# The second block's modulation: sums over partitions by PE transposes and a DVE reduction, two sums in one tied group

## The chip, the cores and the metric

The kernel runs on one core of one Trainium2 chip. The metric is the device time of one launch in microseconds, the median of several runs. The engines are named as the profile does: PE (TensorE matmuls), PEld (its weight loads), DVE (VectorE), ACT (ScalarE), POOL (GpSimd), SP (which starts most DMAs).

## What is computed

Two blocks of two layers each run one after the other over 256 tokens of width 1024, all in fp32. The first block's layers have four mixing branches and a gated feed-forward network. The second block's layers are modulated: the shift, scale and gate vectors come from a conditioning vector `c`, and not from the tokens.

```python
def second_block(x, c, ctx, c_ctx, mod_w, mod_b, ...):
    silu_c = jax.nn.silu(c)                      # (1, 1024)
    silu_cc = jax.nn.silu(c_ctx)
    for i in range(DEPTH):                       # DEPTH = 2
        sh1, sc1, g1, sh2, sc2, g2 = jnp.split((silu_c @ mod_w[i] + mod_b[i])[:, None, :], 6, axis=-1)
        a = modulate(h, norm1_w[i], sh1, sc1)
        if ctx_read:                             # layer 0 alone
            csh1, csc1, cg1, csh2, csc2, cg2 = jnp.split(silu_cc @ mod_w[i] + mod_b[i], 6, axis=-1)
            ac = modulate(hc, norm1_w[i], csh1, csc1)
        ...
```

`mod_w[i]` is 1024 x 6144, so `silu_c @ mod_w[i]` is a product of one row with a large matrix. Only this product is touched here. The context needs the first 2048 of its 6144 columns.

## The kernel before

The kernel is one straight program without loops on the chip. It is recorded operation by operation in Python and then ordered by a scheduler, which weighs every engine's work by a cost model and assigns each instruction its place on its engine's queue. Every queue runs in the order so found. Thus a change to a few instructions can move others far away, on every engine.

Large matrix products (`s_tiles`, `t_form`, with `mm3`) are made of three matmuls each, with weights and tokens split into a high and a low part (lines 483 to 485 and 519 to 521). `weights` (lines 454 to 479) fetches the weights as tiles `w` of 128x1024 (512 KB), ACT casts them to `wh` (line 469) and DVE subtracts to get `wl` (line 470). There are four buffers for `w` and three each for `wh` and `wl`, so these engines can prepare weights ahead of PE.

The product with `mod_w` is made otherwise, beside the first block. `b2_setup` (line 1233) is a generator, and `pump` takes a step of it at each group of matmuls that the first block records, at a rate that depends on the place. It calls `mod_vec` (line 1198): for a block `b` of 512 output columns, eight slices `mw` of `mod_w` (128 rows x 512 columns, two to a DMA) are each multiplied on DVE by a column of `cs`, which holds `silu_c`, and added up in `macc` (lines 1216 and 1218). What is then left is the sum of `macc` over its 128 partitions, and this is wanted as columns: element 128 m + p of the block on partition p, in column m. PE makes it with four matmuls (line 1224), a 128x128 piece of `macc` as weights and one column of ones, into a bank of PSUM, and DVE adds the bias into `mod` or `modc` (line 1226).

There are three calls: layer 0, columns 0 to 2047, for both `c` and the context's vector (four blocks, two accumulators each, `macc0` and `macc1`); layer 0, the other eight blocks, `c` alone (`macc0` alone); layer 1, twelve blocks, `c` alone (`macc0` alone). This makes 28 sums.

The bank comes from `aux2`, of which there are two. The first block takes banks of `aux2` too, for its memory branch (`br_m`) and for the broadcast of the norm's factor (`rstd_bcast`). `macc` buffers are single, so that a block can begin to accumulate in one only when the sum has read it.

At the border of two layers the next layer's norm (lines 437 to 440: `nt`, then `hh` on ACT and `hl` on DVE) needs all of `xT`, so that its first matmuls can't be prepared further ahead than their weights.

Of the kernel before, what the change touches and what calls it, by code (L numbers as in the profile page):

```python
# [3 lines left out]

# [6 lines left out]
F32 = mybir.dt.float32  # L11
# [4 lines left out]
OP = mybir.AluOpType  # L16
AX = mybir.AxisListType
# [231 lines left out]
class K:  # L249
# [948 lines left out]
    def mod_vec(self, i, vecs, blocks, lp):  # L1198

        nc = self.nc  # L1200
        w = self.A["t_mod_w_2"][i]
        for b in blocks:
            accs = [lp.tile([128, 512], F32, tag=f"macc{j}", bufs=1, name="macc") for j in range(len(vecs))]
            for k0 in range(0, KT, 2):
                if k0:
                    yield
                v = lp.tile([128, 2, 512], F32, tag="mw", bufs=2, name="mw")
                self.later(v[:, 0, :1])
                c = TILE_AT["mod_w_2", b * 512][0] + k0 * 128 * 512
                nc.sync.dma_start(v.rearrange("p k n -> p (k n)"),  # L1210
                                  w[c:c + 256 * 512].rearrange("(p n) -> p n", p=128))
                for k in range(2):
                    for acc, (cv, _) in zip(accs, vecs):
                        sc = cv[:, k0 + k:k0 + k + 1]
                        if k0 + k == 0:
                            nc.vector.tensor_scalar(acc, v[:, k, :], sc, None, op0=OP.mult)
                        else:
                            nc.vector.scalar_tensor_tensor(acc, v[:, k, :], sc, acc, op0=OP.mult, op1=OP.add)  # L1218
            yield
            for acc, (_, out) in zip(accs, vecs):  # L1220
                with self.banks("aux2"):
                    ps = self.aux()
                for m in range(4):
                    nc.tensor.matmul(ps[:, m:m + 1], acc[:, m * 128:(m + 1) * 128], self.ones[:, :1], start=True,  # L1224
                                     stop=True)
                nc.vector.tensor_tensor(out[:, b * 4:b * 4 + 4], ps[:, :4], self.col("mod_b_2", i * 48 + b * 4, 4),
                                        OP.add)

    def gain(self, name, i, sc, dst):
        nc = self.nc  # L1230
# [1042 lines left out]
```

## Time and profile before

| | us |
|---|---|
| median of three runs | 1944.95 (1944.28 to 1946.02) |
| the profiled execution | 1944.3 |
| its span, first to last instruction | 1942.5 |
| PE busy | 1905.6 (98%) |
| weight loads busy | 1859.7 (96%) |
| DVE busy | 1479.6 (76%) |
| ACT busy | 1050.7 (54%) |
| granted TensorE clock, mean | 0.994 |

A busy time is the union of an engine's records. Matmul records overlap: each is some 0.28 us long, but the starts of two are about 0.12 us apart, and it is the distance of the starts that tells what one costs in a full stream. A row that stands for several records in a timeline gives their union. A wait is idle time of an engine, put down to what ended last before it went on.

### The profile page before, as it was taken

How to read it: one execution, taken by the hardware profiler on the slowest of the kernel's cores; microseconds unless marked ns; L12 is line 12 of the kernel's file. 1: busy time of each engine (PE TensorE's matmuls, PEld its weight loads, DVE VectorE, ACT ScalarE, POOL GpSimd, SP SyncE). 2: the span in 40 equal slices, each digit the busy share in tenths (PEclk: the TensorE clock that was granted, in tenths of full speed). 3: DMA queues.
4: the chain of work that ended last, by engine and by line, in shares of the span. 5: the costliest groups of instructions: out<-in, count | busy, mean ns of one | idle time of the engine just before them, and what ended most of it. 6: DMA issues, size and time to landing. Idle time of an engine off the chain costs nothing.

```text
span 1942.5 us, 39726 instructions
## 1 busy us (share of the span) xinstructions
PE 1905.6 (98%) x16234; PEld 1859.7 (96%) x16234; DVE 1479.6 (76%) x2362; ACT 1050.7 (54%) x1642; POOL 119.0 (6%) x120
## 2 busy tenths in 40 slices
PE   7999999999999999999999999998999999999998
PEld 7999999999999999999999999997899999899998
DVE  5988987896776879977778966887775557997554
ACT  6664455564644774454555544765254446555443
POOL 0102000110001001000000000000110000010001
PEclk9999999999999999999999999999999999999999
DMA  8865755966567766756653536443146666535653
GB/s 314 290 220 196 243 188 184 308 237 215 182 226 240 266 213 206 242 166 212 244 186 117 188 115 209 150 152 112 63 153 203 195 189 208 178 112 188 193 190 123
DMA packets 118759, 379.63 MB, mean 195 GB/s; under 512 B 18755, under 2 KB 28784, under 8 KB 117296
## 3 DMA queue, kind: packets, MB, share of 16 engines
q1 hardware_dynamic: 117808, 376.44, 57.7%
q8 instruction: 127, 2.08, 0.4%
q0 software_dynamic: 768, 0.66, 0.1%
q14 instruction: 56, 0.46, 0.1%
HBM read 365.94 MB, written 10.25 MB: 194 GB/s over the span
## 4 chain that ended last, share of the span: by engine, by line
PE 88%; DVE 4%; ACT 3%; issue 2%; DMA 1%; POOL 0%; SPq 0%; DVEq 0%; POOLq 0%; ACTq 0%
PE mm L485 23%; PE mm L483 23%; PE mm L484 23%; DVE wl L470 1%; ACT wh L469 1%; PE mm L519 1%; PE aux L1224 1%; PE mm L520 1%; PE mm L521 1%; PE aux L2123 1%; PE aux L2106 1%; PE aux L859 1%; DMA mw<-in_t_mod_w 1%; PE aux L483 1%; PE aux L485 1%
## 5 line engine op out<-in xcount | busy, mean ns | idle before, releaser
L469 ACT CAST wh<-w 128x1024 fp32r<-128x1024 f32 (+2 forms) x570 | 589.0, 1035 | 626.9 <-PE mm L484 473.6
L470 DVE TENSOR_TENSOR wl<-w,wh 128x1024 fp32r<-128x1024 f32 (+2 forms) x570 | 684.4, 1202 | 280.3 <-ACT wh L469 277.7
L483 PE MATMUL mm<-hh,wh 128*128 128x256 f32 (+1 forms) x1776 | 499.9, 282 | 1.4 <-ACT bq L766 0.7
L485 PE MATMUL mm<-hh,wl 128*128 128x256 f32 (+1 forms) x1776 | 499.4, 282 | 1.2 <-DVE wl L470 1.0
L484 PE MATMUL mm<-hl,wh 128*128 128x256 f32 (+1 forms) x1776 | 498.5, 281 | 0.0
L485 PEld LDWEIGHTS mm<-hh,wl 128*128 128x128 f32 (+1 forms) x1776 | 332.6, 187 | 4.1 <-DVE wl L470 1.8
L483 PEld LDWEIGHTS mm<-hh,wh 128*128 128x128 f32 (+1 forms) x1776 | 332.7, 187 | 3.5 <-issue 1.0
L484 PEld LDWEIGHTS mm<-hl,wh 128*128 128x128 f32 (+1 forms) x1776 | 332.3, 187 | 2.4 <-issue 1.8
L485 PE MATMUL mm<-xh,wl 128*128 128x256 f32 x960 | 269.6, 282 | 1.5 <-DVE wl L470 1.5
L483 PE MATMUL mm<-xh,wh 128*128 128x256 f32 x960 | 267.9, 280 | 1.2 <-DVE dqT L1262 0.7
L484 PE MATMUL mm<-xl,wh 128*128 128x256 f32 x960 | 268.6, 281 | 0.2
L485 PE MATMUL mm<-ph,wl 128*128 128x256 f32 x704 | 196.4, 279 | 0.0
L483 PE MATMUL mm<-ph,wh 128*128 128x256 f32 x704 | 195.9, 278 | 0.0
L484 PE MATMUL mm<-pl,wh 128*128 128x256 f32 x704 | 195.8, 278 | 0.0
L485 PEld LDWEIGHTS mm<-xh,wl 128*128 128x128 f32 x960 | 181.1, 189 | 5.1 <-issue 2.6
L483 PEld LDWEIGHTS mm<-xh,wh 128*128 128x128 f32 x960 | 180.8, 189 | 4.1 <-issue 2.7
L484 PEld LDWEIGHTS mm<-xl,wh 128*128 128x128 f32 x960 | 180.6, 189 | 2.9 <-issue 2.2
L1218 DVE SCALAR_TENSOR_TENSOR macc<-mw,cs,macc 128x512 f32<-128x512 f32 x196 | 145.6, 747 | 14.0 <-DMA mw<-in_t_mod_w 13.1
L484 PEld LDWEIGHTS mm<-pl,wh 128*128 128x128 f32 x704 | 132.4, 188 | 0.0
L485 PEld LDWEIGHTS mm<-ph,wl 128*128 128x128 f32 x704 | 132.2, 188 | 0.1
L483 PEld LDWEIGHTS mm<-ph,wh 128*128 128x128 f32 x704 | 132.1, 188 | 0.0
L483 PE MATMUL mm<-brh,wh 128*128 128x256 f32 x384 | 107.9, 281 | 0.0
(705 smaller groups left out, 3478.6 us busy)
## 6 DMA issues: line engine op xcount, KB each, us to landing
w<-in_t_w_in SPq DMA_DIRECT2D x148, 512.0 KB
w<-in_t_ffn_w SPq DMA_DIRECT2D x128, 512.0 KB
mw<-in_t_mod_w SPq DMA_DIRECT2D x96, 512.0 KB
w<-in_t_ffn_w_up SPq DMA_DIRECT2D x88, 512.0 KB
w<-in_t_ab_w_in SPq DMA_DIRECT2D x42, 512.0 KB
w<-in_t_ffn_w_down SPq DMA_DIRECT2D x40, 512.0 KB
w<-in_t_w_lift SPq DMA_DIRECT2D x32, 512.0 KB
w<-in_t_hy_w_in SPq DMA_DIRECT2D x24, 512.0 KB
```

The source lines that it names most:

```text
L469: nc.scalar.copy(wh, w)
L470: nc.vector.tensor_tensor(wl, w, wh, OP.subtract)
L483: nc.tensor.matmul(ps, wh, xh, start=start, stop=False)
L484: nc.tensor.matmul(ps, wh, xl, start=False, stop=False)
L485: nc.tensor.matmul(ps, wl, xh, start=False, stop=stop)
L519: nc.tensor.matmul(o, h, wh, start=(k + tb == 0), stop=False)
L520: nc.tensor.matmul(o, h, wl, start=False, stop=False)
L521: nc.tensor.matmul(o, l, wh, start=False, stop=(k == KT - 1 and tb == 1))
L859: nc.tensor.matmul(ps[:, jj * S:jj * S + ns], qr[r, 2 * jp + jj, tb * 128:(tb + 1) * 128], kr[r, 0, :ns], start=True, stop=True)
L1218: nc.vector.scalar_tensor_tensor(acc, v[:, k, :], sc, acc, op0=OP.mult, op1=OP.add)
L1224: nc.tensor.matmul(ps[:, m:m + 1], acc[:, m * 128:(m + 1) * 128], self.ones[:, :1], start=True, stop=True)
L2106: nc.tensor.matmul(ps, self.Fm[:, c0:c0 + 128], zt[:, part, :], start=True, stop=True)
```

## The change

The four matmuls of a sum become four transposes: the same pieces of `macc` go through PE with the identity, so that in PSUM the 128 partial products of each output column lie along a partition's row, 4 x 128 of them. DVE adds them up there (`tensor_reduce` of 128x4x128 to 128x4, into the column of `mod` or `modc`), and then adds the bias in place.

Sums are made two at a time: `done` collects accumulators until there are two. In the first call a block has two anyway; in the other calls two successive blocks take `macc0` and `macc1` in turn. The eight transposes of a pair are tied by `issue_after`: each may stand on PE only behind the one before it. It does not keep other instructions from standing between them. The later accumulator goes first.

```diff
+        done = []
         for b in blocks:
-            accs = [lp.tile([128, 512], F32, tag=f"macc{j}", bufs=1, name="macc") for j in range(len(vecs))]
+
+            accs = [lp.tile([128, 512], F32, tag=f"macc{j + len(done)}", bufs=1, name="macc")
+                    for j in range(len(vecs))]
             for k0 in range(0, KT, 2):
...
             yield
-            for acc, (_, out) in zip(accs, vecs):
+            done += [(acc, out, b) for acc, (_, out) in zip(accs, vecs)]
+            if len(done) < 2:
+                continue
+            last = None
+            for acc, out, n in done[::-1]:
                 with self.banks("aux2"):
                     ps = self.aux()
                 for m in range(4):
-                    nc.tensor.matmul(ps[:, m:m + 1], acc[:, m * 128:(m + 1) * 128], self.ones[:, :1], start=True,
-                                     stop=True)
-                nc.vector.tensor_tensor(out[:, b * 4:b * 4 + 4], ps[:, :4], self.col("mod_b_2", i * 48 + b * 4, 4),
-                                        OP.add)
+                    with self.tc.issue_after(last) if last is not None else nullcontext():
+                        last = nc.tensor.transpose(ps[:, m * 128:(m + 1) * 128], acc[:, m * 128:(m + 1) * 128],
+                                                   self.ident).ins
+                o = out[:, n * 4:n * 4 + 4]
+                nc.vector.tensor_reduce(o, ps.rearrange("p (m n) -> p m n", m=4), AX.X, OP.add)
+                nc.vector.tensor_tensor(o, o, self.col("mod_b_2", i * 48 + n * 4, 4), OP.add)
+            done = []
```

On PE, the first sum of the program, before (block 1, layer 0; `hh`, `hl` are the tokens' halves, `macc_440` is the accumulator of `c`, and the numbers are those of tiles):

```order
L484 MATMUL mm_968<-hl_760,wh_970 128x256
L485 MATMUL mm_968<-hh_759,wl_971 128x256
L483 MATMUL mm_968<-hh_759,wh_1000 128x256
L484 MATMUL mm_968<-hl_760,wh_1000 128x256
L1224 MATMUL aux_1033<-cst_72,macc_440 128x1 x4
L485 MATMUL mm_968<-hh_759,wl_1001 128x256
```

and now, where `macc_441` is the context's accumulator:

```order
L484 MATMUL mm_968<-hl_760,wh_1000 128x256
L485 MATMUL mm_968<-hh_759,wl_1001 128x256
L1232 MATMUL aux_1033<-cst_72,macc_441 128x128 x4
L1232 MATMUL aux_1040<-cst_72,macc_440 128x128 x4
L483 MATMUL mm_1055<-hh_759,wh_1057 128x256
L484 MATMUL mm_1055<-hl_760,wh_1057 128x256
```

The first sum has moved some twenty matmuls back, to the second one, and both go through PE as one piece, each into a bank of its own.

On DVE at the border between the first block's two layers, before (`nt` and `hl` are the norm of layer 1, `wl` its weights, `mod` and `macc` belong to `mod_vec`):

```order
L1226 TENSOR_TENSOR mod1_81<-aux_7753,P_74 128x4
L1216 TENSOR_SCALAR macc_7759<-mw_7760,cs_437 128x512
L440 TENSOR_TENSOR hl_7689<-nt_7890,hh_7688 128x256
L1218 SCALAR_TENSOR_TENSOR macc_7759<-mw_7760,cs_437,macc_7759 128x512
L470 TENSOR_TENSOR wl_7997<-w_7995,wh_7996 128x1024
L437 SCALAR_TENSOR_TENSOR nt_7902<-xT_73,P_74,upb_7716 128x256
L440 TENSOR_TENSOR hl_7689<-nt_7894,hh_7688 128x256
L440 TENSOR_TENSOR hl_7689<-nt_7898,hh_7688 128x256
L1218 SCALAR_TENSOR_TENSOR macc_7759<-mw_7960,cs_437,macc_7759 128x512
L437 SCALAR_TENSOR_TENSOR nt_7906<-xT_73,P_74,upb_7716 128x256
L437 SCALAR_TENSOR_TENSOR nt_7910<-xT_73,P_74,upb_7716 128x256
L470 TENSOR_TENSOR wl_8036<-w_8034,wh_8035 128x1024
```

and now, to the tile `wl` that answers to the last one above (`wl_8009` and `wl_8048` were `wl_7997` and `wl_8036`):

```order
L470 TENSOR_TENSOR wl_8009<-w_8007,wh_8008 128x1024
L440 TENSOR_TENSOR hl_7707<-nt_7902,hh_7706 128x256
L440 TENSOR_TENSOR hl_7707<-nt_7906,hh_7706 128x256
L440 TENSOR_TENSOR hl_7707<-nt_7910,hh_7706 128x256
L437 SCALAR_TENSOR_TENSOR nt_7914<-xT_73,P_74,upb_7734 128x256
L1235 TENSOR_REDUCE mod1_81<-aux_8263 128x4
L437 SCALAR_TENSOR_TENSOR nt_7918<-xT_73,P_74,upb_7734 128x256
L1235 TENSOR_REDUCE mod1_81<-aux_8270 128x4
L437 SCALAR_TENSOR_TENSOR nt_7922<-xT_73,P_74,upb_7734 128x256
L1219 TENSOR_SCALAR macc_8277<-mw_8278,cs_437 128x512
L470 TENSOR_TENSOR wl_8048<-w_8046,wh_8047 128x1024
```

The accumulation that stood between the norm's pieces is ahead of the border now, but for its first product, and two reductions stand in its place.

## Rows read from the trace of the kernel before

**Rows 1.** The page: busy time of each engine over the span.

```profile
PE 1905.6 (98%) x16234; PEld 1859.7 (96%) x16234; DVE 1479.6 (76%) x2362; ACT 1050.7 (54%) x1642; POOL 119.0 (6%) x120
```

**Rows 2.** The page: the chain that ended last, by line.

```profile
PE mm L485 23%; PE mm L483 23%; PE mm L484 23%; DVE wl L470 1%; ACT wh L469 1%; PE mm L519 1%; PE aux L1224 1%; PE mm L520 1%; PE mm L521 1%; PE aux L2123 1%; PE aux L2106 1%; PE aux L859 1%; DMA mw<-in_t_mod_w 1%; PE aux L483 1%; PE aux L485 1%
```

**Rows 3.** Stretches: us, busy of each engine (records), PE clock, DMA share, GB/s.

```profile
77.00:940.00 863.00, 859.60 (x7074) 838.10 (x7073) 700.74 (x1162) 470.81 (x710) 52.10 (x50) 1.00 0.66 223
940.00:1310.00 370.00, 368.07 (x3378) 365.93 (x3377) 289.77 (x477) 210.54 (x317) 23.64 (x24) 1.00 0.48 163
1310.00:1420.00 110.00, 99.70 (x946) 89.83 (x946) 80.64 (x167) 48.44 (x100) 9.47 (x11) 0.92 0.28 88
```

**Rows 4.** PE's waits in 77 to 940 us: total us, times, longest.

```profile
PE mm L519 <- ACT wh L469: 1.2, 1, 1.2
PE mm L485 <- DVE wl L470: 1.0, 1, 1.0
PE mm L483 <- ACT bq L766: 0.7, 1, 0.7
PE aux L1401 <- DVE lla L1327: 0.3, 1, 0.3
```

**Rows 5.** Line 1224: records, ns min/median/max, first and last start us.

```profile
L1224 PEld LDWEIGHTS aux<-cst,macc x224: 187/192/192, 77.4 to 935.1; 128*128 128x128 f32 x112
L1224 PE MATMUL aux<-cst,macc x224: 164/250/250, 77.5 to 935.1; 128*128 128x1 f32 x112
```

**Rows 6.** Timeline of PE around the first sum: start us, us, instruction.

```profile
77.37 0.28 PE L484 MATMUL mm<-hl,wh 128*128 128x256 f32 x1
77.49 0.95 PE L1224 MATMUL aux<-cst,macc 128*128 128x1 f32 x8
78.30 0.36 PE L485 MATMUL mm<-hh,wl 128*128 128x256 f32 x1
78.50 0.28 PE L483 MATMUL mm<-hh,wh 128*128 128x256 f32 x1
```

**Rows 7.** Line 1539, transposes that the kernel has; columns as in 5.

```profile
L1539 PEld LDWEIGHTS aux<-cst,dkT x16: 138/141/225, 998.5 to 1245.5; 128*128 128x128 f32 x16
L1539 PE MATMUL aux<-cst,dkT x16: 272/272/307, 998.6 to 1245.6; 128*128 128x128 f32 x16
```

**Rows 8.** Timeline of PE around four transposes of line 1539.

```profile
998.49 0.28 PE L485 MATMUL aux<-cxh,wl 128*128 128x256 f32 x1
998.61 0.60 PE L1539 MATMUL aux<-cst,dkT 128*128 128x128 f32 x4
998.97 0.36 PE L485 MATMUL mm<-hh,wl 128*128 128x256 f32 x1
999.17 0.28 PE L483 MATMUL mm<-hh,wh 128*128 128x256 f32 x1
```

**Rows 9.** Stretches: the two microseconds around those transposes.

```profile
998.00:1000.00 2.00, 2.00 (x20) 2.00 (x18) 0.30 (x2) 1.26 (x2) 0.00 (x0) 1.00 0.38 141
```

**Rows 10.** DVE's groups by shape: count, busy us, mean ns, idle before.

```profile
L1064 DVE TENSOR_REDUCE mmx<-aux 128x2 f32<-128x512 f32 x8 | 5.5, 687 | 0.9 <-PE aux L1061 0.9
...
L1226 DVE TENSOR_TENSOR mod<-aux,P 128x4 f32<-128x4 f32 x24 | 3.7, 155 | 3.1 <-PE aux L1224 2.8
```

**Rows 11.** DVE's waits in 77 to 940 us, ACT's over the span.

```profile
DVE wl L470 <- ACT wh L469: 79.3, 81, 3.2
...
ACT wh L469 <- PE mm L484: 473.6, 320, 4.0
```

**Rows 12.** Timeline of DVE at the border of layers.

```profile
641.03 0.15 DVE L1226 TENSOR_TENSOR mod<-aux,P 128x4 f32<-128x4 f32 x1
641.10 0.48 DVE L1216 TENSOR_SCALAR macc<-mw,cs 128x512 f32<-128x512 f32 x1
...
641.83 0.74 DVE L1218 SCALAR_TENSOR_TENSOR macc<-mw,cs,macc 128x512 f32<-128x512 f32 x1
```

**Rows 13.** Stretches: one of the page's 40 slices.

```profile
194.20:242.80 48.60, 48.60 (x394) 46.78 (x393) 45.35 (x93) 21.87 (x29) 0.00 (x0) 1.00 0.73 242
```

More of the change, by code (lines that the diff above doesn't have):

```diff
@@ L1 @@
 import math
-from contextlib import ExitStack, contextmanager
+from contextlib import nullcontext, ExitStack, contextmanager
 from itertools import chain
```

## The prediction

> **What bounds the kernel now.** I read the page's busy line and the chain first: TensorE (PE) is busy 1905.6 of 1942.5 us, and the weight matmuls of lines 483 to 485 are 69% of the chain that ended last, with line 1224, the one that the change replaces, at 1% [rows 1, 2]. Then the table of stretches, to see whether that holds where the change lies. Line 1224 runs from 77.4 to 935.1 us [rows 5]. In 77 to 940 us PE is busy 859.6 of 863.0 us at a granted clock of 1.00, that is 2.4 GHz; VectorE (DVE) is busy 700.7 and the DMA engines 66% [rows 3]. PE's waits of that stretch are four single ones, 1.2 us the longest, 3.2 us together [rows 4]. So what PE no longer has to execute there ends the kernel earlier by as much, unless something new makes PE wait.
>
> **The change part by part.** *The sums on PE.* There are 28 sums: 4 blocks with two vectors, then 8 and 12 blocks with one. Each was 4 matmuls, a 128x128 piece of `macc` as weights and one column of ones. The records say 224 matmuls for these 112 [rows 5], so each fp32 matmul costs two passes with two weight loads. Price of one sum from the stream of starts: the last ordinary matmul before it starts at 77.37, the second one after it at 78.50, 1.13 us, of which two ordinary steps of 0.115 would have passed anyway: 0.90 us [rows 6]. That is 8 records at 0.11 us.
>
> Now each sum is 4 transposes. The same form stands in the kernel already, in line 1539: 16 transposes in the code and 16 records, one pass each, with weight loads of 141 ns instead of 192 [rows 5, 7]. Four of them in the same kind of stream: 998.49 to 999.17, 0.68 us, less two steps of 0.12: 0.44 us [rows 8]. Nothing is paid to enter or leave the group beyond the 0.11 us for each record. One sum therefore saves 0.90 - 0.44 = 0.46 us; the rows are good to a few hundredths, and I take 0.45: 28 x 0.45 = **12.6 us**. The nearest ends are 0.42 and 0.47, 11.8 to 13.2 us.
>
> *Two sums tied.* Half of the 14 pairs stand as eight transposes in a row in the new order, the others as two pieces. Since a transpose costs the same 0.11 us wherever it stands, I put the tie itself at nothing on PE. What it does hold is both `aux2` banks at once. Ahead of a pair, whoever needs `aux2` (the memory branch, the norms' broadcasts) waits for both reductions. No PE wait of 77 to 940 us names such a bank [rows 4]; it goes into the layout term below.
>
> *DVE.* It gains 28 reductions of 128x512 from PSUM into 128x4. The line-1064 reduction has this input size and source and takes 687 ns: 28 x 0.687 = 19.2 us. The small bias addition stays, 155 ns, reading SBUF instead of PSUM [rows 10]. What hides the 19.2 us: DVE stands idle 79.3 us in this stretch for ScalarE's (ACT) casts `wh`, and ACT in turn, over the span, waits 473.6 us for PE to release a weight buffer [rows 11]. The weight splitting thus runs ahead of PE as far as its three buffers allow, and a reduction of 0.7 us in front of a `wl` is absorbed. I take 0; the bounds are 0 and all 19.2 us.
>
> *The layer boundary.* At about 640 us the lead is gone, because the norm of the next layer needs the whole of `xT`. Two of PE's four waits are there, 1.0 us for `wl` and 1.2 us for `wh` [rows 4]. Between the norm's pieces DVE does modulation work: up to the last `wl` of the order shown a bias addition, a first product and two further ones, 0.15 + 0.48 + 2 x 0.74 = 2.1 us [rows 12]. The new order has two reductions and one first product ahead of the same `wl`, 0.69 + 0.69 + 0.48 = 1.9 us [rows 10, 12]: two accumulators alternate now, so much of the next block's accumulation has moved ahead, under the last matmuls of the layer before. I take 0 net; both waits could vanish (-2.2 us) or each grow by a reduction (+1.4 us).
>
> *The layout.* The scheduler weighs the whole program anew. From the first pair on every queue is rearranged, SP's weight loads too; only the last 4327 PE instructions, from the end of the stretch 1310 to 1420 us on, stand in the old order. In 77 to 1310 us PE now idles 3.4 + 1.9 = 5.3 us [rows 3]. A new layout should have about as much: I take 0, with -3 us if most of it closes and +9 us if a dozen waits of the present kind (3.2 us in four, 0.8 each, rows 4) come on top. The idle and slow-clock stretch, 1310 to 1420 us, 99.7 of 110.0 us busy at clock 0.92 [rows 3], has its PE instructions rearranged in short pieces only, and holds none of the sums. I take 0 there too; a third of its 10.3 idle us either way, 3 us, is the bound.
>
> *Clock.* Around the four transposes of line 1539 the granted clock stays 1.00 and PE is busy 2.00 of 2.00 us [rows 9]. The Trainium skill speaks against the change here: its page "TensorE: Matmul & The Clock Gate", section "Part 4: PE-mode transpose", says that the full clock does not engage for transposes. By that rule the groups would run at the lower level and the saving would be gone; by the row nothing is lost. The row is a group of four and the change makes eights, so a rival below keeps a small chance.
>
> **Sum.** The profiled execution took 1944.3 us, 1.8 more than its span; the median of the three runs is 1944.95, 0.65 above it. 1944.3 - 12.6 = 1931.7; the same step from the median gives 1932.35, and I say **1932.4 us**.
>
> **The rivals.**
>
> 1. *Gain partly returned to new waits.* For it: every queue is laid anew, and the pairs hold both `aux2` banks. Against it: four waits in 863 us now, and buffers that run ahead [rows 4, 11]. Six to eight new waits of 0.8 us are about 6 us: 1938.4; a dozen 1942.
> 2. *DVE becomes the bound (slower).* Its place is where both engines are full: DVE is busy 45.35 of 48.60 us in the slice at 194 us, PE all of it [rows 13]. Every reduction that delays a `wl` that PE is waiting for costs 0.687 us. The change is a loss once more than 12.6 / 0.687, 18 of the 28, do so; all 28 give 1932.4 + 19.2 = 1951.6. Against it: over the whole stretch DVE has 162 us left [rows 3], half of that as waits for casts [rows 11].
> 3. *The transposes do not come cheaper.* If the eights pull the clock to its lower level, 1.2 GHz, a transpose takes 0.22 us, the group of four 0.88 and the saving is 28 x 0.02, under 1 us: 1944.4. If instead the transposes came as two passes, the same. Against both: one record each, at clock 1.00 [rows 7, 9].
> 4. *A luckier layout.* The boundary waits close and some of the other idle time too, -2.2 and -3: 1927.2.
>
> **Chances.** The forecast, 1929.5 to 1935.5: 0.60. Rival 1, 1935.5 to 1946: 0.22. Rival 2, 1946 and more: 0.08. Rival 3, about 1944.4: 0.04. Rival 4, below 1929.5: 0.06. A measurement of this kernel can tell 0.2%, 3.9 us, from no change, so faster means below 1941.1. That is the forecast, rival 4 and about half of rival 1: 0.60 + 0.06 + 0.11 = 0.77. The same is the other half less a little, and rival 3: 0.13. Slower is rival 2 with the tail of rival 1: 0.10. The range leaves out rival 2, half of rival 4 and the upper part of rival 1: 1928.5 to 1943.
>
> **What would show it.** The sums' line should have 112 records instead of 224, weight loads near 141 ns, and 0.44 us for four in the stream of starts. The reduction should take 0.68 to 0.69 us, 28 times. PE in 77 to 940 us of before should do the same ordinary matmuls in about 850 us, with idle time of 3 to 4 us. If DVE was the limit, PE's waits for `wl` would grow from 1.0 us to ten or more. If the clock was, the stretches would show less than 1.00 there. If the layout was, the waits would be many and spread over unlike lines. I would be wrong by the size of a term if a sum in the new stream cost more than 0.5 us.

## The result and the profile after

| | before | after |
|---|---|---|
| median, us | 1945.49 (1944.28 to 1948.18) | 1972.0 (1968.95 to 1974.87) |
| ratio, 95% interval | | 1.0128 [1.0115, 1.0142] |
| span of the profiled execution, us | 1942.5 | 1970.3 |

The change makes the kernel 26.5 us slower by the medians, 24.9 us by the ratio. The forecast was 1932.4 us, so the prediction was wrong, and in its sign. This is the page of the changed kernel, busy lines ([rows 1] has that of before) and slices of 49 us:

```profile
span 1970.3 us, 39529 instructions
PE 1912.0 (97%) x16122; PEld 1860.3 (94%) x16122; DVE 1496.4 (76%) x2390; ACT 1054.8 (54%) x1646; POOL 119.5 (6%) x120
PE   8999999899999999999999999999999999999998
PEclk9999999899999999999999999998999999999999
```

PE has 112 records fewer, as foreseen, and is yet busy 6.4 us longer, and idle 58.3 us instead of 36.9. Two things thus stand against each other: the sums got cheaper, and PE lost 21.4 us to waits and, if 12.6 us of work went as estimated, about 19 us to the same work done at longer steps. Together, 21.4 + 19.0 - 12.6, this is the 27.8 us by which the span grew. The granted clock says much the same of the steps: 0.006 of 1942.5 us was not granted before and 0.015 of 1970.3 us after, 18 us more. The eighth slice, 345 to 394 us, shows both, a lower share of PE and a lower clock.

The edited instructions themselves did just what was foreseen. Their own records, by line (duration min/median/max, first and last start):

```profile
L1232 PEld LDWEIGHTS aux<-cst,macc x112: 138/140/143, 79.5 to 976.4; 128*128 128x128 f32 x112
L1232 PE MATMUL aux<-cst,macc x112: 270/272/328, 79.6 to 976.5; 128*128 128x128 f32 x112
```

The reduction among the groups (busy, mean ns, idle before):

```profile
L1235 DVE TENSOR_REDUCE mod<-aux 128x4 f32<-128x512 f32 x24 | 16.1, 685 | 5.0 <-PE aux L1232 5.0
```

The first tied pair in the timeline of PE:

```profile
79.46 0.28 PE L485 MATMUL mm<-hh,wl 128*128 128x256 f32 x1
79.58 1.04 PE L1232 MATMUL aux<-cst,macc 128*128 128x128 f32 x8
80.37 0.36 PE L483 MATMUL mm<-hh,wh 128*128 128x256 f32 x1
80.57 0.28 PE L484 MATMUL mm<-hl,wh 128*128 128x256 f32 x1
```

and the table of stretches around it:

```profile
79.00:81.00 2.00, 2.00 (x20) 2.00 (x19) 0.57 (x1) 1.97 (x3) 0.00 (x0) 1.00 1.00 383
```

From 79.46 to 80.57 are 1.11 us; less two ordinary steps of 0.115, eight transposes cost 0.88, twice the 0.44 of [rows 8], at a granted clock of 1.00.

Where the loss lies shows in PE's waits in 77 to 940 us, where PE is now idle 24.5 us (total us, times, longest, as in [rows 4], where the four waits of before make 3.2 us):

```profile
PE aux L877 <- DVE blg L872: 5.7, 2, 4.8
PE mm L485 <- DVE wl L470: 4.2, 6, 2.0
PE mm L483 <- ACT bq L766: 3.7, 2, 2.1
PE mm L483 <- ACT ax L724: 2.6, 1, 2.6
```

and in two stretches (columns as in [rows 3]), after:

```profile
330.00:400.00 70.00, 60.84 (x424) 54.68 (x423) 47.07 (x76) 34.95 (x56) 0.69 (x1) 0.88 0.63 217
640.00:800.00 160.00, 150.01 (x1215) 147.24 (x1214) 134.83 (x218) 92.47 (x142) 13.19 (x16) 0.96 0.72 243
```

and before, when PE had both at the full clock:

```profile
330.00:400.00 70.00, 70.00 (x577) 67.86 (x575) 57.73 (x92) 39.24 (x58) 10.88 (x3) 1.00 0.84 285
640.00:800.00 160.00, 157.06 (x1314) 153.62 (x1314) 139.09 (x240) 98.70 (x148) 11.81 (x15) 1.00 0.67 223
```

The first of these stretches is the end of the sparse attention of the first block's first layer (`br_b`). That attention is a long chain in which each step needs the one before: index scores on DVE (line 832), two sets of eight selection rounds on DVE (lines 837 and 838: the eight largest, then strike them out), then eight steps of logits on PE (859), DVE (863 to 866), ACT (869), DVE (871, 872), PE (877) and ACT, and last the lift of the result, which is the last thing the layer's mixing part needs. While it runs, PE works on other products of the layer (gates, lifts, projections), and there is only a finite stock of them. PE's timeline in the changed kernel, toward the chain's end:

```profile
365.27 0.39 PE L485 MATMUL mm<-hh,wl 128*128 128x256 f32 x1
365.48 0.29 PE L483 MATMUL mm<-hh,wh 128*128 128x256 f32 x1
...
366.16 1.13 PE L859 MATMUL aux<-bk,bq 64*128 64x256 f32 x4
372.13 1.09 PE L877 MATMUL aux<-cst,blg 128*128 128x128 f32 x4 [4.84 <-DVE blg L872]
...
379.22 0.41 PE L484 MATMUL mm<-brl,wh 128*128 128x256 f32 x1
379.43 0.41 PE L485 MATMUL mm<-brh,wl 128*128 128x256 f32 x1
```

and the stretch:

```profile
366.00:380.00 14.00, 8.48 (x30) 5.40 (x28) 6.77 (x14) 5.04 (x10) 0.00 (x0) 0.60 0.23 74
```

PE has sent off the last logits, and its queue holds nothing else ahead of line 877: it waits 4.84 us, for a weight split that stands first on DVE and then for DVE's and ACT's part of that one step. After the wait the matmuls start 0.21 us apart instead of 0.12. The granted clock is 0.50, its lower level of 1.2 GHz, from 368.9 us, inside the wait, to 382.4. So an idle stretch is paid twice, once as a wait and once as slow steps behind it.

The last step itself is not slow. These are its first and last work on DVE, after and then before:

```profile
368.14 0.68 DVE L863 TENSOR_TENSOR blg<-aux,bbias 128x512 f32<-128x512 f32 x1
371.29 0.69 DVE L872 TENSOR_TENSOR blg<-blg,bsm 128x512 f32<-128x512 f32 x1
```

```profile
335.95 0.69 DVE L863 TENSOR_TENSOR blg<-aux,bbias 128x512 f32<-128x512 f32 x1 [0.60 <-PE aux L859]
346.01 0.69 DVE L872 TENSOR_TENSOR blg<-blg,bsm 128x512 f32<-128x512 f32 x1
```

It took 3.8 us after the change and 10.8 before, with five accumulations in it; but before, PE had other products for that time. What the change lacks is the stock: the step comes 32 us later, when PE has used it up.

Why is the chain late? Here is DVE in the changed kernel, in the middle of the index scores and the first selection rounds:

```profile
230.09 0.75 DVE L1221 SCALAR_TENSOR_TENSOR macc<-mw,cs,macc 128x512 f32<-128x512 f32 x1
230.76 0.48 DVE L832 SCALAR_TENSOR_TENSOR bsc<-brl__2104,biw,bsc 128x256 f32<-128x256 f32 x1
231.16 0.29 DVE L837 MAX8 m<-bsc 128x8 f32<-128x128 f32 x1
231.60 1.23 DVE L470 TENSOR_TENSOR wl<-w,wh 128x1024 fp32r<-128x1024 f32 x1 [0.16 <-ACT wh L469]
232.74 0.75 DVE L1221 SCALAR_TENSOR_TENSOR macc<-mw,cs,macc 128x512 f32<-128x512 f32 x1
233.40 0.48 DVE L832 SCALAR_TENSOR_TENSOR bsc<-brl__2111,biw,bsc 128x256 f32<-128x256 f32 x1
233.80 0.09 DVE L838 MATCH_VALUE_LOAD bsc<-m,bsc 128x8 f32 x1
233.87 0.28 DVE L838 MATCH_REPLACE8 bsc<-m,bsc 128x128 f32<-128x128 f32 x1
```

A selection round of 0.3 us stands behind an accumulation of the modulation (0.75 us) and a weight split (1.2 us), again and again. Before, the single accumulator kept the modulation in check there: a block's last accumulation started at 254.7 us, and the next block could start only when the sum had read `macc0`, at 315.8 us, behind most of the logits. With pairs there are two accumulators in turn, and the next block goes straight on. Between the first selection round and the eighth logits DVE does 27 accumulations before and 38 after; DVE's part of the eighth logits (line 863) starts at 335.9 us before and at 368.1 after.

The accumulations alone do not make up this delay. The sixteen selection rounds take 17.8 us longer, and DVE's accumulations among them went from 10.1 to 14.2 us. Weight splits went from 14 to 19 there, 6.0 us more, and the rest is other work of DVE and idle time. The splits come at the same pace in both, one in 3.2 or 3.3 us, so a chain that is stretched takes in more of them; that this is how a few accumulations grow to the whole delay is my reading, and no run tests it by itself.

### The profile page after: what moved, and what is told of

Read it like the earlier page. It is cut to its first block, busy times and chain, and to the rows that moved or that the text cites. A ratio compares the mean times of both kernels' runs of the same rounds, so it can differ in the third digit from the quotient of the medians.

```text
span 1970.3 us, 39529 instructions
## 1 busy us (share of the span) xinstructions
PE 1912.0 (97%) x16122; PEld 1860.3 (94%) x16122; DVE 1496.4 (76%) x2390; ACT 1054.8 (54%) x1646; POOL 119.5 (6%) x120
## 4 chain that ended last, share of the span: by engine, by line
PE 81%; DVE 7%; ACT 5%; issue 3%; DMA 3%; POOL 0%; SPq 0%; DVEq 0%; POOLq 0%; ACTq 0%
PE mm L483 22%; PE mm L485 22%; PE mm L484 22%; DVE wl L470 2%; ACT wh L469 2%; DMA mw<-in_t_mod_w 1%; DVE macc L1221 1%; PE aux L2133 1%; PE aux L2116 1%; PE aux L859 1%; PE aux L483 1%; PE aux L484 1%; PE aux L485 1%; DMA tok<-in_mem 1%; PE aux L1232 1%
## 5 line engine op out<-in xcount | busy, mean ns | idle before, releaser
L483 PEld LDWEIGHTS mm<-hh,wh 128*128 128x128 f32 (+1 forms) x1776 | 337.0, 190 | 13.5 <-ACT bq L766 4.2
L485 PEld LDWEIGHTS mm<-hh,wl 128*128 128x128 f32 (+1 forms) x1776 | 336.6, 190 | 6.2 <-DVE wl L470 4.8
L484 PEld LDWEIGHTS mm<-hl,wh 128*128 128x128 f32 (+1 forms) x1776 | 336.7, 190 | 2.4 <-issue 1.0
```

The lines of the kernel that those rows point to most:

```text
L483: nc.tensor.matmul(ps, wh, xh, start=start, stop=False)
L484: nc.tensor.matmul(ps, wh, xl, start=False, stop=False)
L485: nc.tensor.matmul(ps, wl, xh, start=False, stop=stop)
```

## The experiments

All ratios are to the kernel before in the same set of runs, with 95% intervals. *Theory A*: the second accumulator lets the modulation into the latency chains, PE runs dry, and this, not the price of the sums, decides. *Rival D*: the 28 reductions overload DVE. *Rival T*: the tie of the pairs costs. *Rival L*: any new order is worse than the old one, which is a tuned one. (In the texts of the first four runs, theory B is the reductions, D here, and theory C is L.)

This table holds what the traces of the runs say of the two places. Selection: from the first to the sixteenth selection round of layer 0, its duration and the accumulations in it, in brackets those up to the eighth logits. The eighth logits are taken at DVE's line 863, the last gate at its last product in layer 0 (line 1134). Stretch: from the first feed-forward product of layer 0 to that of layer 1 (DVE line 553). The traces of m_alt and no_sum are of executions 8.6 us faster than the medians, so their rows show a part of the loss only.

| kernel | ratio | accumulations | selection, us | 8th logits at | last gate of layer 0 at | stretch, us |
|---|---|---|---|---|---|---|
| before | 1 | 16 (27) | 45.4 | 335.9 | 383.0 | 564.8 |
| after | 1.0128 | 22 (38) | 63.2 | 368.1 | 396.7 | 576.0 |
| t_single | 0.9987 | 16 (28) | 49.3 | 340.6 | 384.6 | 561.8 |
| m_pair | 1.0092 | 19 (29) | 53.0 | 343.7 | 386.8 | 583.3 |
| m_alt | 1.0118 | 21 (37) | 58.5 | 347.3 | 388.1 | 578.9 |
| t_alt | 1.0104 | 20 (42) | 61.0 | 363.4 | 393.2 | 578.6 |
| before_r0 | 1.0071 | 0 (2) | 32.9 | 315.3 | 386.5 | 565.2 |
| after_r0 | 1.0030 | 0 (0) | 30.1 | 296.6 | 379.5 | 567.5 |
| no_sum | 1.0124 | 24 (63) | 59.5 | 368.5 | 402.3 | 547.7 |
| t_nored | 0.9962 | 11 (24) | 43.2 | 338.0 | 383.6 | 564.0 |
| pair_first | 1.0078 | 22 (38) | 63.1 | 368.3 | 396.6 | 563.4 |
| pair_second | 1.0030 | 16 (30) | 52.1 | 349.4 | 383.9 | 578.5 |

### The parts of the change, one at a time

**t_single**: transposes and reductions, one sum at a time, one accumulator as before.

```diff
-                    nc.tensor.matmul(ps[:, m:m + 1], acc[:, m * 128:(m + 1) * 128], self.ones[:, :1], ...)
-                nc.vector.tensor_tensor(out[:, b * 4:b * 4 + 4], ps[:, :4], self.col("mod_b_2", ...), OP.add)
+                    nc.tensor.transpose(ps[:, m * 128:(m + 1) * 128], acc[:, m * 128:(m + 1) * 128], self.ident)
+                o = out[:, b * 4:b * 4 + 4]
+                nc.vector.tensor_reduce(o, ps.rearrange("p (m n) -> p m n", m=4), AX.X, OP.add)
+                nc.vector.tensor_tensor(o, o, self.col("mod_b_2", i * 48 + b * 4, 4), OP.add)
```

> The transposes and the DVE reduction alone: each sum is made as soon as its accumulator is full, the later blocks keep one accumulator, no pairs. Theory A (the loss comes from the second accumulator: accumulation runs on without waiting for a sum and crowds DVE while the sparse attention selects its keys): the order has 16 accumulation steps between the first and the sixteenth of the selection rounds, as before (the change has 22), so the price on PE comes through: 1930 to 1937 us. Theory B (the 28 reductions overload DVE): as slow as the change, 1955 to 1975. Theory C (any new layout costs by chance): anywhere between 1930 and 1975.

**m_pair**: the change without transposes; the sums are matmuls with ones, in tied pairs on two accumulators.

```diff
-                        last = nc.tensor.transpose(ps[:, m * 128:(m + 1) * 128], ...).ins
+                        last = nc.tensor.matmul(ps[:, m:m + 1], acc[:, m * 128:(m + 1) * 128], self.ones[:, :1], ...).ins
```

> The pairs alone: two sums at a time, tied, accumulators in turn, but each sum by the old four matmuls and the one addition. Theory A: slower than before, 1955 to 1980 us, since the second accumulator is there; the order has 19 accumulation steps in the selection rounds, between 16 and 22, so rather the lower half. Theory B: no loss, 1943 to 1948, since there are no reductions. Theory C: anywhere.

**m_alt**: the kernel before, its one-vector blocks on two accumulators in turn; no pairs, no tie, no transposes.

```diff
-tag=f"macc{j}"
+tag=f"macc{(j + b) % 2}"
```

> Two accumulators in turn alone: the old sums, one at a time, but each block takes the other accumulator than the block before it. Theory A: slow, 1960 to 1985 us (21 accumulation steps in the selection rounds, 37 up to the last logits, nearly the 22 and 38 of the change), and the last logits of layer 0 about 30 us later than before. Theory B: 1943 to 1948. Theory C: anywhere.

**t_alt**: t_single with the same edit of the accumulators.

> Transposes and reductions one at a time, with two accumulators in turn: against t_single this adds the second accumulator alone. Theory A: slow, 1955 to 1980 us (20 and 42 accumulation steps), against 1930 to 1937 of t_single. Theory B: slow like t_single. Theory C: anywhere.

Measured: t_single 0.9987 [0.9977, 0.9996], m_pair 1.0092 [1.0074, 1.0111], m_alt 1.0118 [1.0092, 1.0143], t_alt 1.0104 [1.0088, 1.0120]. One edited expression, the second accumulator, makes 1.2% without any of the rest; in m_pair and m_alt more of it lies in the stretch between the feed-forward parts (18 and 14 us) than at the attention (the last gate 4 and 5 us late), which theory A did not foresee. Rivals D and T fall as the cause: with all reductions and no second accumulator nothing is lost, and m_alt has neither reductions nor ties. But t_single gains 2.5 us where PE executes 12.6 us less, and theory A's 1930 to 1937 us for it was missed. Its page:

```profile
PE 1896.9 (98%) x16122; PEld 1848.7 (95%) x16122; DVE 1495.1 (77%) x2390; ACT 1052.7 (54%) x1644; POOL 118.2 (6%) x120
```

and the two stretches:

```profile
330.00:400.00 70.00, 66.66 (x536) 63.50 (x535) 57.27 (x95) 40.00 (x59) 5.04 (x3) 0.98 0.76 276
640.00:800.00 160.00, 154.81 (x1289) 150.68 (x1289) 140.85 (x237) 97.85 (x149) 12.01 (x15) 1.00 0.69 223
```

PE is busy 8.7 us less than before and idle 46.4 us of 1943.3, 9.5 more. Most of the saved time came back as waits, 3.3 us of them at the end of the attention.

### The chain cleared of accumulations

`pump` hands out modulation steps at a rate for each part of the kernel. With the mixing part's rate lower, the scheduler leaves the chain nearly free.

**before_r0**, **after_r0**, **tsing_r0** (t_single):

```diff
-RATES = (0, 0.9, 0.5, 0.9, 2)
+RATES = (0, 0.3, 0.5, 0.9, 2)
```

> The kernel before with one number changed: the rate at which a layer's mixing part hands out modulation steps is 0.3 instead of 0.9. In the new order no accumulation stands on DVE between the first and the sixteenth selection round of either layer (before 16 and 14), and 2 instead of 27 up to the eighth logits of layer 0. Theory A (accumulations between the selection rounds delay the sparse attention, and PE runs dry when it waits for that): the eighth logits of layer 0 start some 15 to 20 us earlier than 335.95 us; but before had PE full at that place, so the time falls little, 1938 to 1946 us. Rival L (the loss is in the order as a whole, whichever it is): the time goes to 1955 and more, as for the two-accumulator kernels.

> The whole change, with the rate 0.3 instead of 0.9. No accumulation stands in either layer's selection any more (after 22 in layer 0), none up to the eighth logits (after 38). Theory A: the 26.5 us loss is gone, at least most of it: 1930 to 1942 us, with the eighth logits before 345 us instead of at 368 and PE idle in 330 to 400 us below 1 us instead of 9.2. Rival L (two accumulators or the tie cost by themselves, or any new order does): 1960 us and more. Rival D (the 28 reductions cost DVE 19 us that PE waits for): 1950 to 1960 us.

> Transposes and reductions one sum at a time on one accumulator, with the rate 0.3. Theory A: 10 to 13 us under the kernel before with rate 0.3, since the PE time saved (12.6 us) is no longer eaten by a wait for the sparse attention; and within 4 us of the whole change with rate 0.3. Rival D: within 3 us of the kernel before with rate 0.3, as the transposes at rate 0.9 were within 0.13% of before. Rival T (the tie and the pairs cost by themselves): 10 us and more under the whole change at rate 0.3.

**after_r2**: `RATES = (0, 0.3, 1.5, 1.5, 2)` in the changed kernel.

> The whole change with rates 0.3 in the mixing part, 1.5 after the sparse attention and 1.5 in the feed-forward part (0.9, 0.5, 0.9 before). The selections are again free of accumulations, but the layer 0 feed-forward part and the start of layer 1 hold 176 accumulations on DVE instead of 96 in the whole change at rate 0.3. Theory A, with DVE's room of 180 us after 400 us: within 4 us of the whole change at rate 0.3. If the loss of 11 us at the layer boundary (658 to 702 us) comes from accumulations crowding DVE there too, it is 8 to 15 us slower than that.

Measured: before_r0 1.0071 [1.0047, 1.0095], after_r0 1.0030 [1.0015, 1.0046], tsing_r0 1.0050 [1.0034, 1.0066], after_r2 1.0245 [1.0225, 1.0265]. The local part of theory A came out: without accumulations the sixteen rounds take 30 to 33 us instead of 45 (before) and 63 (after), and the hole at the chain's end is gone. after_r0 at that place:

```profile
330.00:400.00 70.00, 68.54 (x573) 66.97 (x573) 66.78 (x112) 41.96 (x57) 1.50 (x4) 1.00 0.78 261
```

The last gate of layer 0 comes at 379.5 us, 3.5 before that of before, and the changed kernel is here faster than the unchanged one at the same rate, by 0.4% (1954.15 against 1961.68 us). Theory A's totals were missed in all four runs all the same. after_r0 took 1954 us and not 1930 to 1942: 80 accumulations are left for behind layer 1's attention, and the part from the first feed-forward product of layer 1 to the last work on DVE takes 959 us instead of 951. before_r0 came out as rival L said, 1962 us and not 1938 to 1946. tsing_r0 was to be 10 to 13 us under before_r0 and is 3.7 under it (1958.0 us), so with a free chain, too, most of the 12.6 us saved on PE does not arrive. after_r2 shows the other wall: with 176 accumulations pressed between the attentions, PE waits 14.7 us in one piece for `macc` itself, and is busy only 205.7 of the 240 us from 400 to 640; it is 41 us above after_r0, where the most that I had given was 15.

### How much of it is any shift of the order

**before_80** and **before_ff80**: the kernel before, one rate moved a notch, the same work.

```diff
-RATES = (0, 0.9, 0.5, 0.9, 2)
+RATES = (0, 0.8, 0.5, 0.9, 2)      (before_80)
+RATES = (0, 0.9, 0.5, 0.8, 2)      (before_ff80)
```

> The kernel before with the mixing part's rate 0.8 instead of 0.9: one accumulator, the old sums, the same work, only the place of the modulation steps moves a little. It holds 14 and 26 accumulations in layer 0's selection and up to the eighth logits (before 16 and 27). Theory L (the order of before is a tuned one, and any other order of the same work costs some tenths of a per cent to one per cent, spread over the layer boundary and the second layer): 1950 to 1965 us. Theory A alone (only accumulations in the selection chain cost): 1943 to 1948 us.

> The kernel before with the feed-forward part's rate 0.8 instead of 0.9. The order is the old one up to the layer 0 feed-forward part, so layer 0's attention must come out as before (eighth logits at 335.9 us, the first product of the feed-forward part at 421.6 us). In layer 1's selection there are fewer accumulations than before (8 instead of 14, up to the logits' end 10 instead of 24). Theory L: still 5 to 15 us slower, arising after 570 us. Theory A alone: the same time or a few us less.

**tsing_early**: t_single with `R0 = 0.3` instead of 0.2. **after_early**: the change with `R0 = 0.5` and `RATES = (0, 0.5, 0.5, 1.1, 2)`.

> Transposes and reductions one sum at a time on one accumulator, with the modulation's rate ahead of the first layer 0.3 instead of 0.2, so that more of it is done before the selection: 8 and 20 accumulations in the chain instead of 16 and 28. Theory A: the eighth logits come before 340.6 us and the first product of the feed-forward part some 5 to 10 us before 423.6, and unless the layer boundary takes it back the kernel gains against before: 1934 to 1942 us. Theory L: any loss behind the boundary is as likely as not to take it back, 1943 to 1958 us.

> The whole change with the rates 0.5 ahead of the first layer, 0.5 in the mixing part and 1.1 in the feed-forward part (0.2, 0.9, 0.9 before). No accumulation stands in either selection chain; 80 instead of 74 are done before the first one. Theory A: layer 0's first product of the feed-forward part comes at 415 to 425 us instead of 440.7. In all: 1935 to 1950 us by A, if the rest of the order is no worse than at rate 0.3 (1954 us with 80 accumulations left for the second block; here 48 are left, which should give some of that back). Theory L: 1950 to 1970 us.

Measured: before_80 1.0038 [1.0026, 1.0050], before_ff80 1.0029 [1.0020, 1.0039], tsing_early 0.9989 [0.9977, 1.0001], after_early 1.0033 [1.0018, 1.0048]. before_ff80 kept layer 0 as it was (eighth logits at 335.3 us) and lost 11 us behind it, as L said; in tsing_early the first feed-forward product came at 423.0 us, no earlier than in t_single, against A. All four times lie where L had them, and none where A had; after_early took 1955.0 us and not 1935 to 1950. Rival L is true to this size: the same work in a slightly shifted order is 0.3 to 0.4% slower (0.7% for before_r0), 6 to 8 us, so the old order is a good one among its neighbours. None of these shifts reaches 1.3%. after_early has no accumulations in either chain and its last gate of layer 0 at 377.3 us, 19 us before the change as it was made, and still ends above before.

### Is the chain cause or company?

**no_sum**: the kernel before with the sums taken off PE altogether. The sum over the 128 partitions is left out.

```diff
-                for m in range(4):
-                    nc.tensor.matmul(ps[:, m:m + 1], acc[:, m * 128:(m + 1) * 128], self.ones[:, :1], ...)
-                nc.vector.tensor_tensor(out[:, b * 4:b * 4 + 4], ps[:, :4], ...)
+                nc.vector.tensor_tensor(out[:, b * 4:b * 4 + 4], acc[:, :4], ...)
```

> The kernel before without its 28 sums over the partitions: the bias addition reads four columns of the accumulator instead, so the modulation's values are wrong and the sum's work is left out. PE executes 28 x 0.90 = 25 us less, DVE gains nothing. But the accumulator is free at once, and 63 instead of 27 accumulations now stand on DVE in layer 0's chain up to the eighth logits, 24 instead of 16 in the selection. If PE is the bound (the prediction's ground): 1920 us, 1916 to 1926. Theory A: the eighth logits come some 36 x 0.74 = 27 us later than 335.95, 355 to 370 us; PE idles there, and the time is 1935 to 1965 us in spite of 25 us less work.

**t_nored**: t_single without the reductions; the sum over 128 products is left out.

```diff
-                nc.vector.tensor_reduce(o, ps.rearrange("p (m n) -> p m n", m=4), AX.X, OP.add)
-                nc.vector.tensor_tensor(o, o, ...)
+                nc.vector.tensor_tensor(out[:, b * 4:b * 4 + 4], ps[:, :4], ...)
```

> Transposes one sum at a time on one accumulator, without the reductions: the bias addition reads the first four columns of the transposed tile, so the sum over 128 products is left out. PE saves its 12.6 us, DVE gains nothing. 11 and 24 accumulations in the chain (16 and 28 with the reductions). Rival D (the reductions on DVE ate the saving): 1932 to 1936 us, 10 us below the kernel with the reductions, 1945.2. Theory A and L (PE is not what sets the end where the sums lie, and orders differ by some tenths of a per cent): 1938 to 1950 us.

Measured: no_sum 1.0124 [1.0099, 1.0149], t_nored 0.9962 [0.9947, 0.9977]. no_sum is the plainest of the runs: PE has some 25 us less to do, DVE nothing more, and the kernel is 24 us slower, above even the 1935 to 1965 us that A had given. Nothing now holds the accumulations back. The timeline of DVE in no_sum, with accumulations inside and around a logit step:

```profile
360.76 1.53 DVE L1218 SCALAR_TENSOR_TENSOR macc<-mw,cs,macc 128x512 f32<-128x512 f32 x2
362.32 0.16 DVE L1221 TENSOR_TENSOR mod<-macc,P 128x4 f32<-128x4 f32 x1
362.90 0.42 DVE L863 TENSOR_TENSOR blg<-aux,bbias 128x256 f32<-128x256 f32 x1 [0.41 <-PE aux L859]
363.36 0.42 DVE L865 TENSOR_REDUCE bmx<-blg 128x2 f32<-128x256 f32 x1
363.82 0.49 DVE L1216 TENSOR_SCALAR macc<-mw,cs 128x512 f32<-128x512 f32 x1
```

PE's wait for the eighth step stands in the next line. It is put down to the modulation's bias addition (line 1221 of that kernel), which ends 0.07 us behind the step's own last part; five accumulations and a weight split stand inside the step:

```profile
PE aux L877 <- DVE mod L1221: 5.7, 1, 5.7
```

and the stretch:

```profile
330.00:400.00 70.00, 61.42 (x435) 54.73 (x434) 58.38 (x96) 34.15 (x56) 0.69 (x1) 0.90 0.80 272
```

The hole in 330 to 400 us has the size and the clock of the change's. From the last gate to the first feed-forward product, with 17 accumulations there, no_sum takes 59.9 us (38.6 in before, with none), and the stretch behind that gives 17.1 us back. In t_nored 7.4 of the 12.6 us arrive, 2.5 in t_single, as A and L had it: the reductions take some 5 us (the two intervals together leave 1 to 8), though the two orders also differ by 4 accumulations in the chain, so that this is a size for both together.

**after_paced** and **before_paced**: both kernels with `R0 = 0.5` and `RATES = (0, 0.6, 0.8, 1.1, 2)`.

> The whole change with the modulation's rates 0.5 ahead of the first layer, 0.6 in the mixing part, 0.8 behind the sparse attention and 1.1 in the feed-forward part (0.2, 0.9, 0.5, 0.9 before). No accumulation stands in a selection chain, and only 16 are left behind layer 1's, as in the change as it was made. Theory A: layer 0's first feed-forward product at 414 to 422 us (440.7 in the change), layer 1's at 985 to 1000 us (1016.7), the end at 1940 to 1952 us.

> The kernel before with the same rates as the paced change (0.5, 0.6, 0.8, 1.1): one accumulator and the old sums. 6 and 14 accumulations in layer 0's chain (before 16 and 27), none in layer 1's. Together with the paced change it shows what the change does where the chain is nearly free in both: theory A says the paced change is 5 to 13 us faster than this, since the PE time it saves is then not eaten by the wait for the attention. Theory L for this run: 1950 to 1960 us, as for the other shifted orders of before.

Measured: 1.0039 [1.0018, 1.0060] and 1.0051 [1.0036, 1.0066]. The changed kernel is 2 us under the other, which these runs can't tell from nothing. That is below the 5 expected, and the change's own numbers were missed too: layer 0's first feed-forward product came at 433.6 us, not at 414 to 422, and the end at 1960.5, with 8.3 us of waits and a clock of 0.94 in 640 to 800 us. The last gate is early, at 381.0 us; but the rate of 0.8 puts 14 accumulations between it and the first feed-forward product, which takes 52.6 us instead of 38.6. So even where the chain is free, most of the saving does not arrive.

### The second place

**pair_first** and **pair_second**: the change with pairs in the first 16 sums only, or in the last 12 only; the others one at a time on one accumulator.

```diff
-            if len(done) < 2:
+            if len(done) < (1 if i else 2):      (pair_first)
+            if len(done) < (2 if i else 1):      (pair_second)
```

> The whole change, but only the first vector set (the modulation of layer 0 of the second block, 16 of 28 sums) is summed in pairs on two accumulators; the 12 sums of the second are done one at a time on one accumulator. DVE's chain of layer 0 is that of the change (22 and 38 accumulations), layer 1's that of the single sums (16 and 32). Theory A: the last gate of layer 0 comes at 396 us as in the change (396.7; 384.6 with single sums). If the loss at the layer boundary comes from the pairs there, the stretch from the first feed-forward product of layer 0 to that of layer 1 takes 562 us as with single sums (576 in the change) and the time is 1957 to 1963 us. If it comes from the late layer 0 or from the order in general, the stretch takes 570 and more: 1965 to 1975 us.

> The other half: the 16 sums of the first set one at a time on one accumulator, the 12 of the second in pairs on two. Layer 0's chain is nearly that of the single sums (16 and 30 accumulations), layer 1's that of the change (none). Theory A: the last gate of layer 0 at 384 to 386 us. If the pairs cost at the layer boundary, the stretch between the two feed-forward parts takes 573 to 585 us and the time is 1953 to 1965 us. If the boundary's loss only follows from the late layer 0, the stretch takes 562 us and the time is 1943 to 1948 us.

Measured: pair_first 1.0078 [1.0063, 1.0093], pair_second 1.0030 [1.0018, 1.0041]; both came as expected if the pairs cost at the layer boundary. The two stretches of both, the first fence pair_first, the second pair_second:

```profile
330.00:400.00 70.00, 61.08 (x440) 54.93 (x439) 48.97 (x80) 35.78 (x57) 0.69 (x1) 0.90 0.65 223
640.00:800.00 160.00, 154.81 (x1300) 151.98 (x1299) 135.05 (x216) 98.57 (x150) 12.70 (x16) 1.00 0.68 223
```

```profile
330.00:400.00 70.00, 69.21 (x552) 64.99 (x551) 62.03 (x108) 43.81 (x65) 8.69 (x6) 1.00 0.80 280
640.00:800.00 160.00, 149.86 (x1200) 145.10 (x1199) 139.32 (x236) 94.20 (x144) 12.71 (x15) 0.97 0.69 227
```

and PE's waits of pair_second in 640 to 800 us:

```profile
PE mm L483 <- ACT ax L724: 2.6, 1, 2.6
PE mm L483 <- ACT bq L766: 2.1, 1, 2.1
```

The loss splits cleanly. Pairs in the first half make the hole at the attention's end (13% of 330 to 400 us idle and a low clock) and leave 640 to 800 us as in t_single (154.81 us busy in both; that the hundredths agree is luck). Pairs in the second half leave the attention alone and make the loss in 640 to 800 us, with the very waits of the change (2.6 us for `ax`, 2.1 for `bq`). In sums, against t_single: 17.7 us for the first half, 8.4 us for the second, each good to some 3 us, and with t_single's -2.5 that is 23.6 us of the 24.9 that the change's ratio stands for.

An accumulation in a chain need not cost much. Layer 1's selection holds 14 in before, 16 in t_single and in pair_first, and none in the change. From its first round to 20 us behind its eighth logits PE is idle 0.0, 1.6, 1.7 and 0.0 us. What an accumulation costs thus depends on how much other work PE has left there.

## Why the prediction was wrong, step by step

*The price of a sum on PE* was right: 112 records, weight loads of 140 ns, 0.44 us for four. The Trainium skill's page "TensorE: Matmul & The Clock Gate", section "Part 4: PE-mode transpose", would have had the transposes at the lower clock; the pair at 79.6 us, eight of them between ordinary matmuls, ran at 1.00, so the measurement decides against that rule here. No run has transposes without matmuls around them.

*The reductions* were right in price, 685 ns, and their cover was too kindly judged: 0 taken, some 5 us measured, inside the bounds of 0 and 19.2. Rival 2 was priced against the weight splits alone, and its sign, waits for `wl` of ten us or more, did not come: they are 4.2 us on line 485. DVE's 162 us of room was an average over 863 us; in the attention's selection rounds DVE is idle 5.0 of 63.2 us.

*The tie* was not run by itself. The rows don't need it: m_alt and t_alt have no tie and lose 1.2 and 1.0%. What the change loses beyond t_alt, 0.2%, may be the tie or the order.

*The layer boundary and the layout* are where the prediction failed: both terms were 0, with bounds of +1.4 and +9 us, and 21.4 us of new waits and some 19 us of slow steps came. "Two accumulators alternate now, so much of the next block's accumulation has moved ahead" was the right observation with the wrong sign. I counted the moved accumulations as work taken away from behind (0 net) and did not ask what they were moved in front of. They were moved from behind the sum into the selection rounds of layer 0's attention; the pairs there cost 17.7 us. The pairs of the second half cost 8.4 us, in the opening of layer 1; that it is the moved accumulations there, too, is not shown. My places were [rows 4, 12 and 13], that is the waits that the old order had. The old order had no wait at the attention's end, so that place had no row. The bound of the layout rested on "a dozen waits of the present kind". The wait at the attention's end was of another kind, 4.8 us long and followed by slow steps. In 640 to 800 us two of the old waits grew, for `wl` from 1.0 to 2.0 us and for `bq` from 0.7 to 2.1, and one of 2.6 us for `ax` came in, with the same slow steps behind them (clock 0.96).

*"What PE no longer has to execute there ends the kernel earlier by as much"* failed too, and by itself: t_single and t_nored cost PE 12.6 us less and gain 2.5 and 7.4. 859.6 of 863 us busy [rows 3] did not say that PE was the bound there. At the attention it said that a finite stock of other products was just long enough to fill the time that the chain takes on DVE and ACT. Where the stock is just used up at the chain's end, PE work taken from the stock turns into a wait: in t_single the last gate comes at 384.6 us, no earlier than before (383.0), and PE is idle 3.3 us in 330 to 400, where it was not idle before.

*The clock*, put at 0, cost 18 to 19 us in the end by the two estimates above, though not by the transposes: the steps behind PE's waits are slow.

*What I had said would show the layout to be at fault*, many waits over unlike lines, is part of what came (before_80 and its like put 0.3 to 0.7% on that), but the largest share is two places, and in the change both go with the second accumulator.

What stays open: by which instruction the second half's accumulations make PE wait for `ax` and `bq` in layer 1. In the 40 us behind that layer's norm DVE does 10 or 11 accumulations in before, t_single, t_nored and pair_first and 14 to 17 in the five kernels with pairs or two accumulators there; but before_80 has 16 as well and loses only 2.5 us in that stretch, so the count alone is not the answer. No kernel here beat before by 0.2% or more, apart from t_nored, which leaves work out.

## What to carry to other kernels

A buffer that is "only" single may be what paces background work: before giving it a second copy, or making its release earlier, look which latency chain on the same engine its producer will then be scheduled into, and count the instructions between the chain's links in the new order, the chain's other company as well. A busy share of 98% shows a bound only if work would be left over; ask how long the chain that ends the stage takes without it, and test that by taking work out of the engine altogether. Judge a reorder against shifted orders of the old kernel too, since a tuned order can be several tenths of a per cent better than its neighbours.

## What the runs showed of the hardware that I had not expected

The granted clock fell with waits of a few microseconds, and this is paid for afterwards. In the changed kernel's wait of 4.84 us, which ended at 372.1 us, it fell to 0.50 (1.2 GHz) at 368.9, and it stayed there for 10 us behind the wait, with matmuls 0.21 us apart. Even two shorter waits in close order, 1.02 us that ended at 360.4 and 0.76 at 361.6, were followed by steps of 0.21 us up to 365.3 (0.53 in 361.9 to 365.4). Two others, 0.82 us that ended at 353.1 and 0.48 at 354.2, were not: 350 to 358 us is at 1.00.
